# The last three modulation vectors of a DiT layer as products on ScalarE and sums on GpSimd

## The chip, the cores and the metric

The kernel runs on one core of one Trainium2 chip. The metric is the time of one execution on the device in microseconds (us). TensorE multiplies matrices, VectorE and ScalarE work on rows of up to 128 partitions, GpSimd (POOL in the profile) does element-wise work here, and SyncE (SP) issues nearly all DMAs. Each engine executes its own list of instructions in order.

## What is computed

One layer of a diffusion backbone: a feed-forward sublayer (FFN), a mixer (a gated delta rule beside windowed attention), and a second FFN, each with a norm that is shifted, scaled and gated by modulation vectors. Two groups of tokens go through it, 128 of a prompt and 512 of a sample, each with its own conditioning vector. All data is fp32. What the change touches:

```python
mod_p = (jax.nn.silu(c_ctx) @ ada_w[l] + ada_b[l])[None, None, :]
mod_s = (jax.nn.silu(c) @ ada_w[l] + ada_b[l])[:, None, :]
sh1p, sc1p, g1p, sh2p, sc2p, g2p, sh3p, sc3p, g3p = jnp.split(mod_p, N_MOD, axis=-1)
...
xp = ffn_sublayer(xp, norm_ffn1[l], sh1p, sc1p, g1p, ffn1_w13[l], ffn1_w2[l])
...
xp = xp + g2p * merge_branches(y_a, y_b, gate_raw, w_oa[l], w_ob[l], w_out[l])
xp = ffn_sublayer(xp, norm_ffn2[l], sh3p, sc3p, g3p, ffn2_w13[l], ffn2_w2[l])
```

`ada_w` has 1024 rows and 9 x 1024 columns, 4 MB for each of the nine vectors. Vectors 0 and 1 (shift and scale of the first FFN) are needed at once, 2 after the first round, 3 and 4 before the mixer, 5 at its end, and 6, 7 and 8 only in the second FFN.

## The kernel before

The FFN (`ffn`) has 22 column tiles f of 128 columns, in six rounds (0-2, 3-6, 7-10, 11-13, 14-17, 18-21). In a round each column tile makes one tile of the hidden layer, and then the second product runs over eight output tiles d and adds to the residual `X` (L455). The column tiles from f = 3 on use `product_pair` (L203): two weight blocks a and b of 512 KB are loaded (`load`, L115, three `wraw` buffers), GpSimd makes four sums and differences of their halves (`ss`, L580 to L583, four buffers), and each weight is split into a high part on ScalarE (`wh` or `sh`, L127) and a rest on VectorE (`wl` or `sl`, L128). Then seven products of twelve matmuls run over 320 columns each: 84 matmuls to a pair. In the names below, `big` and `aux` are PSUM tiles (two and four).

The modulation vectors 2 to 8 are made by a generator (`rest`, with `modulation`) that `ffn` advances through `between`: by two steps behind each of the first two column tiles, by one behind every other, and by one behind each four output tiles d in the rounds but the last. A step loads two blocks of 128 rows x 1024 columns (`araw`, L273, 512 KB each, a ring of two buffers), multiplies them with the 32 columns that repeat the two conditioning vectors (`s32`), and adds the result to `modr` (L286, L288):

```python
for g in range(4):
    nc.tensor.matmul(
        ps[32 * g : 32 * g + 32],
        lhsT=self.s32[:, k, :],
        rhs=raw[:, g * 256 : (g + 1) * 256],
```

The four matmuls of a block write four strips of 32 rows of one PSUM tile. The trace counts each of them as two instructions (two passes). After four steps a vector is complete and is transposed (L292), given its bias and kept in `mod` (L293). The 28 steps end in the fifth round. A scheduler writes the order of each engine's instructions from the order in the code, priorities and its own model of times; on the chip each engine follows that list and waits for semaphores.

Of the kernel before, what the change touches and what calls it, by code (L numbers as in the profile page):

```python
# [10 lines left out]
F32 = mybir.dt.float32  # L11
# [3 lines left out]
AF = mybir.ActivationFunctionType  # L15
ALU = mybir.AluOpType
# [3 lines left out]
P = 128  # L20
D = 1024
# [65 lines left out]
def flat(t):  # L87
    return t.rearrange("p a b -> p (a b)")
# [10 lines left out]
class Net:  # L99
# [147 lines left out]
    def vectors(self):  # L247
        nc = self.nc
        c = self.const
        ps = self.aux_tile()  # L250
        nc.tensor.transpose(ps[:, 0:16], self.crows, self.ident[0:16, 0:16])
        sT = self.tile(c, [P, 16], F32, "sT")
        nc.scalar.activation(sT, ps[:, 0:16], AF.Silu)
        self.s32 = self.tile(c, [P, KD, 32], F32, "s32")
        for v in range(2):
            nc.vector.tensor_copy(
                self.s32.rearrange("p k (r v) -> p v k r", v=2)[:, v],
                sT[:, v * 8 : v * 8 + 8].unsqueeze(2).to_broadcast([P, KD, 16]),
            )
        ps = self.aux_tile()  # L260
        nc.tensor.transpose(ps[:, 0:105], self.vrows[0:105], self.ident[0:105, 0:105])
        self.vecT = self.tile(c, [P, 105], F32, "vecT")
        nc.vector.tensor_copy(self.vecT, ps[:, 0:105])
        self.mod = self.tile(c, [P, 9, KD, 2], F32, "mod")

    def modulation(self, m):


        nc, a = self.nc, self.a
        r = self.tile(self.small, [P, 256], F32, "modr", 2)  # L270
        for k in range(KD):
            raw = self.tile(self.apool, [P, D], F32, "araw", 2)
            nc.sync.dma_start(raw, a["ada_w"][0, k * P : (k + 1) * P, m * D : (m + 1) * D])  # L273
            if k % 2 == 0:
                ps = self.aux_tile()[:, 0:256]
# [5 lines that stand above are left out]
                    start=(k % 2 == 0),  # L281
                    stop=(k % 2 == 1),
                )
            if k % 2:
                if k == 1:
                    nc.vector.tensor_copy(r, ps)  # L286
                else:
                    nc.vector.tensor_tensor(r, r, ps, op=ALU.add)  # L288
                yield
        p2 = self.aux_tile()  # L290
        for h in range(2):
            nc.tensor.transpose(p2[:, h * P : (h + 1) * P], r[:, h * P : (h + 1) * P], self.ident)  # L292
        nc.vector.tensor_tensor(  # L293
            self.mod[:, m].rearrange("p (g h) v -> p g h v", h=2),
            p2[:, 0:256].rearrange("p (h g r) -> p g h r", h=2, g=4)[:, :, :, 0:2],
            self.vecT[:, m * 8 : m * 8 + 8]
            .rearrange("p (g h) -> p g h", h=2)
            .unsqueeze(3)
            .to_broadcast([P, 4, 2, 2]),
            op=ALU.add,  # L300
        )

    def modulation_part(self, m0, d0, nd):

# [1121 lines left out]
    def build(self):  # L1426
        nc, a, tc = self.nc, self.a, self.tc
# [4 lines left out]
        def pool(name, **k):  # L1432
            return tc.tile_pool(name=name, bufs=1, reuse_waits="tile", **k)

        def dram(shape, tag):
            return self.tile(self.dram, shape, F32, tag)

        with (
# [9 lines left out]
            with (  # L1448
# [7 lines left out]
                with pool("ada0", side="right") as ada, ExitStack() as inner:  # L1456
                    with pool("in1", side="right") as self.phase:
                        self.load_input(xall, ss)
                        r = self.token_rstd(ss)
# [50 lines left out]
                with pool("g1", side="right") as self.phase:  # L1510
                    gates = {m: self.tile(self.const, [P, KD, 2], F32, f"gate{m}") for m in (2, 5, 8)}

                    def rest():
                        for m in range(2, 9):
                            yield from self.modulation(m)
                            if m in gates:
                                nc.vector.tensor_scalar(gates[m], self.mod[:, m], 0.5, None, op0=ALU.mult)
                        self.scale_columns(4, 80, A2)
                        self.scale_columns(7, 88, A3)
                        self.constants_late()  # L1520

                    A2, A3 = (self.tile(self.const, [P, KD, 2], F32, tag) for tag in ("A2", "A3"))
                    steps = rest()

                    def between(n):
                        for _ in range(n):
                            next(steps, None)

                    last = self.ffn(hs, X, gates[2], a["ffn1_w13"][0], a["ffn1_w2"][0], self.phase, between=between, first=first)
                    hs = self.next_operands(last, X, A2, 3)  # L1530
                    xd = dram([KD, P, T], "xd")
                    for d in range(KD):
                        nc.sync.dma_start(xd[d], flat(X[d]))


            with ExitStack() as right:
# [8 lines left out]
                with pool("mixt") as tmp, pool("attn") as at:  # L1545
# [29 lines left out]
                rest = [  # L1575
                    lambda off=off, chain=chain: list(chain(self.product(self.wcols(a["w_in"][0], off), hs)))
                    for off, chain in zs[2:]
                ]

                op = right.enter_context(pool("o", side="right"))  # L1580
                self.oT = self.tile(op, [P, H_A, T], F32, "oT")
                with pool("prep") as pp, pool("scan") as sp:
                    self.delta(pp, sp, rest)
                    self.nfill, self.fill = 160, 0
                    self.gates(stage, hs, range(16))
                    yB = []
                    for r in range(4):
                        t = self.tile(stage, [P, 2, HT], F32, "stage", 2)
                        nc.sync.dma_start(flat(t), ybd[r])
                        yB.append(self.operand(t, self.operand_tiles(1)[0]))  # L1590
                    tB = self.branch_b(stage, yB)
                    self.nfill = 0
# [11 lines left out]
                with pool("x2") as xpool:  # L1604
# [13 lines left out]
                    with pool("g2", side="right") as self.phase:  # L1618
                        last = self.ffn(hs, X, gates[8], a["ffn2_w13"][0], a["ffn2_w2"][0], self.phase, weight=self.vecT[:, 97:105])
                        acc = next(last)  # L1620
# [36 lines left out]
```

## Time and profile before

| | |
|---|---|
| median of 3 runs | 1578.33 us (1575.17 to 1578.99) |
| the profiled execution | 1579.08 us |
| its span in the profile | 1577.4 us |
| mean granted TensorE clock | 0.989 of full speed (2.4 GHz) |
| first FFN with its modulation steps, about | 50 to 485 us of the span |
| second FFN, about | 1150 to 1560 us of the span |

A view of the profile names an instruction by line, engine, operation and tiles (out<-in). PE is TensorE's matmul, PEld its weight load, DVE VectorE, ACT ScalarE, SPq the DMA queue of SyncE. The chain of waits is the chain of work that ended last, followed back from the end of the program.

### The profile page before, as it was taken

To read this page: it belongs to the slowest core of one execution; us is meant where nothing else is said; L and a number is where in the kernel's file an instruction comes from. 1 tells how busy PE (TensorE), PEld (TensorE's weight loads), DVE (VectorE), ACT (ScalarE), POOL (GpSimd) and SP (SyncE) were. 2 spreads that over 40 slices of the span, in tenths; PEclk is the share of its full clock that TensorE was granted. 3 is DMA by queue.
4 is the path that set the end of the run, shared out by engine and by line. 5 is a ranking of instruction groups with operands and counts; after the bars stand their busy time and mean duration, and the time that the engine had idled before them with its cause. 6 is when DMAs were issued, how large, how long until landed. Compare 5 with 4: busy or idle time off the path is not lost.

```text
span 1577.4 us, 28409 instructions
## 1 busy us (share of the span) xinstructions
PE 1537.0 (97%) x11210; PEld 1458.9 (92%) x11210; DVE 1091.9 (69%) x2309; ACT 657.7 (42%) x1214; POOL 293.6 (19%) x240
## 2 busy tenths in 40 slices
PE   6999999999999899999999999999999999999998
PEld 4889999989999798788999999999899999999997
DVE  5877575658576758976765655765698776677676
ACT  4434232324243546564455544323353333334244
POOL 1022221222220110100321122000014141241410
PEclk8999999999999999999999999999999999999999
DMA  9654354445325341214533323445022313223122
GB/s 304 206 170 160 129 173 146 134 146 170 94 80 137 93 129 44 66 41 126 177 111 98 103 80 123 152 140 164 24 75 73 116 57 109 68 68 107 55 81 67
DMA packets 219119, 181.15 MB, mean 115 GB/s; under 512 B 16032, under 2 KB 194397, under 8 KB 218987
## 3 DMA queue, kind: packets, MB, share of 16 engines
q1 hardware_dynamic: 218731, 179.29, 37.2%
q8 instruction: 88, 1.44, 0.4%
q14 instruction: 44, 0.36, 0.1%
q0 software_dynamic: 256, 0.06, 0.0%
HBM read 161.59 MB, written 16.42 MB: 113 GB/s over the span
## 4 chain that ended last, share of the span: by engine, by line
PE 84%; DVE 7%; DMA 3%; ACT 2%; issue 2%; POOL 1%; SPq 0%; DVEq 0%; POOLq 0%; ACTq 0%
PE big L173 31%; PE aux L203 21%; PE aux L173 10%; PE aux L160 9%; PE big L203 8%; DMA wraw<-ffn_w 2%; DVE wl L128 1%; PE aux L277 1%; DVE x L455 1%; PE aux L157 1%; DVE sl L128 1%; ACT wh L127 1%; DVE cacc L870 1%; PE aux L317 1%; POOL ss L580 1%
## 5 line engine op out<-in xcount | busy, mean ns | idle before, releaser
L127 ACT CAST wh<-wraw 128x1024 fp32r<-128x1024 f32 (+1 forms) x147 | 150.6, 1027 | 270.0 <-PE big L173 89.9
L128 DVE TENSOR_TENSOR wl<-wraw,wh 128x1024 fp32r<-128x1024 f32 (+1 forms) x147 | 183.0, 1247 | 84.1 <-ACT wh L127 80.9
L173 PE MATMUL big<-hh,wh 128*128 128x320 f32 x768 | 192.9, 322 | 8.7 <-ACT hh L351 3.3
L173 PE MATMUL big<-hl,wh 128*128 128x320 f32 x768 | 192.3, 321 | 0.6 <-DVE hl L420 0.5
L173 PE MATMUL big<-hh,wl 128*128 128x320 f32 x768 | 188.1, 318 | 0.5 <-DVE wl L128 0.4
L580 POOL TENSOR_TENSOR ss<-wraw 128x512 f32<-128x512 f32 x38 | 51.2, 1349 | 725.3 <-DMA wraw<-ffn_w 648.6
L127 ACT CAST sh<-ss 128x512 fp32r<-128x512 f32 x152 | 92.7, 620 | 186.1 <-POOL ss L581 89.2
L128 DVE TENSOR_TENSOR sl<-ss,sh 128x512 fp32r<-128x512 f32 x152 | 133.2, 884 | 44.6 <-ACT sh L127 43.8
L173 PEld LDWEIGHTS big<-hh,wh 128*128 128x128 f32 x768 | 131.1, 191 | 15.1 <-ACT hh L351 5.5
L203 PE MATMUL aux<-th,sh 128*128 128x320 f32 x456 | 141.7, 311 | 2.2 <-DVE x L455 2.2
L203 PE MATMUL aux<-tl,sh 128*128 128x320 f32 x456 | 141.5, 310 | 0.0
L203 PE MATMUL aux<-th,sl 128*128 128x320 f32 x456 | 141.4, 310 | 0.0
L173 PEld LDWEIGHTS big<-hl,wh 128*128 128x128 f32 x768 | 131.3, 191 | 6.6 <-DVE hl L420 3.3
L173 PEld LDWEIGHTS big<-hh,wl 128*128 128x128 f32 x768 | 131.9, 191 | 3.3 <-issue 2.2
L455 DVE SCALAR_TENSOR_TENSOR x<-big,gate,x 128x128 f32<-128x128 f32 (+2 forms) x181 | 67.5, 424 | 36.4 <-PE big L173 36.1
L203 PEld LDWEIGHTS aux<-th,sh 128*128 128x128 f32 x456 | 86.2, 189 | 2.7 <-DVE x L455 2.7
L173 PE MATMUL big<-gh,wh 128*128 128x320 f32 x352 | 88.5, 313 | 0.0
L173 PE MATMUL big<-gl,wh 128*128 128x320 f32 x352 | 87.7, 310 | 0.0
L173 PE MATMUL big<-gh,wl 128*128 128x320 f32 x352 | 87.1, 309 | 0.0
L203 PEld LDWEIGHTS aux<-tl,sh 128*128 128x128 f32 x456 | 86.2, 189 | 0.0
L203 PEld LDWEIGHTS aux<-th,sl 128*128 128x128 f32 x456 | 86.2, 189 | 0.0
L1066 DVE TENSOR_TENSOR P<-aux,lv 128x512 f16<-128x512 f32 x70 | 48.2, 689 | 46.8 <-PE aux L160 46.8
(378 smaller groups left out, 3919.4 us busy)
## 6 DMA issues: line engine op xcount, KB each, us to landing
wraw<-ffn_w SPq DMA_DIRECT2D x116, 512.0 KB, 4.0
araw<-ada_w SPq DMA_DIRECT2D x64, 512.0 KB, 5.7
wraw<-w_in SPq DMA_DIRECT2D x35, 512.0 KB, 4.0
wraw<-ffn_w SPq DMA_DIRECT2D x16, 384.0 KB, 3.3
gd<-stage SPq DMA_DIRECT2D x16, 320.0 KB, 2.7
araw<-ada_w SPq DMA_DIRECT2D x16, 256.0 KB, 6.0
wraw<-w_out SPq DMA_DIRECT2D x8, 512.0 KB, 4.2
xd<-x SPq DMA_DIRECT2D x8, 320.0 KB, 2.2
```

The costliest lines, as they stand in the source:

```text
L127: nc.scalar.copy(hi, raw)
L128: nc.vector.tensor_sub(lo, raw, hi.bitcast(F32))
L157: self.marks.append(self.nc.tensor.transpose(*args))
L160: self.marks.append(self.nc.tensor.matmul(*args, **kw))
L173: self.nc.tensor.matmul(ps[h], lhsT=wt[:, k, c0 : c0 + P], rhs=xt[:, h, :], start=(k == 0 and j == 0), stop=(k == len(xs) - 1 and j == 2),)
L203: nc.tensor.matmul(ps, lhsT=wt[:, k * P : (k + 1) * P], rhs=xt, start=(k == 0 and j == 0), stop=(k == n - 1 and j == 2),)
L277: nc.tensor.matmul(ps[32 * g : 32 * g + 32], lhsT=self.s32[:, k, :], rhs=raw[:, g * 256 : (g + 1) * 256], start=(k % 2 == 0), stop=(k % 2 ...
L317: last = nc.tensor.matmul(ps[32 * j : 32 * j + 32], lhsT=self.s32[:, 2 * q + k, :], rhs=raw[:, k, m, :], start=(q == 0), stop=(q == 3),)
L455: nc.vector.scalar_tensor_tensor(X[:, h, cols], ps[:, cols], gate[:, d, v : v + 1], X[:, h, cols], op0=ALU.mult, op1=ALU.add)
L580: nc.gpsimd.tensor_tensor(f[0], b[:, :n], b[:, n:], op=ALU.add)
L870: nc.vector.scalar_tensor_tensor(acc, buf[:, t : t + n], w, acc, op0=ALU.mult, op1=ALU.add)
L1066: mark = nc.vector.tensor_tensor(P16, p1, mask, op=ALU.mult)
```

## The change

Vectors 2 to 5 are made as before. For 6, 7 and 8 a second generator (`rest_sums`, with `modulation_sums`) runs beside the first: `between` advances it by one step whenever it is called with 1. One block g of 256 columns of a vector takes two steps; a step loads 512 rows of it as one `araw` tile (128 partitions x 4 x 256, in the same ring of two buffers). ScalarE multiplies each of the four 128 x 256 pieces by its conditioning value per partition, once for each of the two conditioning vectors, and GpSimd adds the results up in `macc`; `mprod`, which holds a product, and `macc` have one buffer each. At the end of a block TensorE sums over the 128 partitions with two matmuls (one for each conditioning vector, with a mask of zeros and ones as the stationary operand) into the strip of 32 rows of block g, VectorE copies the strip to `modr`, and the rest is as before. In the first FFN the `sh` and `sl` buffers go from six to five, as the second FFN has them already. The late constants are loaded after vector 5 instead of after vector 8.

```diff
     def modulation(self, m):
...
+        self.modulation_vector(m, r)
+
+    def modulation_vector(self, m, r):
...
+    def modulation_sums(self, m):
+        nc, a = self.nc, self.a
+        r = self.tile(self.small, [P, 256], F32, "modr", 2)
+        for g in range(4):
+            acc = self.tile(self.phase, [P, 2, 256], F32, "macc", 1)
+            for q in range(2):
+                raw = self.tile(self.apool, [P, 4, 256], F32, "araw", 2)
+                src = a["ada_w"][0, q * 512 : (q + 1) * 512, m * D + g * 256 : m * D + (g + 1) * 256]
+                nc.sync.dma_start(raw, src.rearrange("(k p) f -> p k f", p=P))
+                for k in range(4):
+                    t = acc if q == 0 and k == 0 else self.tile(self.phase, [P, 2, 256], F32, "mprod", 1)
+                    for v in range(2):
+                        nc.scalar.activation(
+                            t[:, v], raw[:, k], AF.Copy, scale=self.s32[:, 4 * q + k, v : v + 1]
+                        )
+                    if t is not acc:
+                        nc.gpsimd.tensor_tensor(acc, acc, t, op=ALU.add)
+                yield
+            ps = self.aux_tile()[:, 0:256]
+            for v in range(2):
+                nc.tensor.matmul(
+                    ps[32 * g : 32 * g + 32], lhsT=self.pick[:, v], rhs=acc[:, v], start=(v == 0), stop=(v == 1)
+                )
+            rows = slice(32 * g, 32 * g + 32)
+            nc.vector.tensor_copy(r[rows], ps[rows])
+        self.modulation_vector(m, r)
...
-                        for m in range(2, 9):
+                        for m in range(2, 6):
                             yield from self.modulation(m)
...
+                    def rest_sums():
+                        for m in range(6, 9):
+                            yield from self.modulation_sums(m)
...
                     def between(n):
                         for _ in range(n):
                             next(steps, None)
+                        if n == 1:
+                            next(sums, None)
+                    self.nsh = 5
```

Line numbers in the rows of the changed kernel are higher: L277 is the load of a modulation step, L281 its matmul, L321 the load of a sum's step, L325 a product, L329 an addition, L333 the matmul over partitions, and L617 to L620 are the four operations of a pair on GpSimd. In the waits, PE, Activation, DVE and Pool are the engines waited for; DMAHW is an earlier DMA.

SyncE in the third round (column tiles f = 8 and 9), before: two `araw` loads to a step, both waiting for TensorE.

```order
L273 DMA araw_2192<-ada_w 128x1024 [waits DMAHW4_49,DMAHW0_49,PE_49]
L273 DMA araw_2199<-ada_w 128x1024 [waits DMAHW1_49,PE_49]
L115 DMA wraw_2525<-ffn_w 128x8x128 [waits DVE_49,Pool_49]
L115 DMA wraw_2527<-ffn_w 128x8x128 [waits DMAHW2_49,DVE_49,Pool_49]
L273 DMA araw_2350<-ada_w 128x1024 [waits DMAHW4_49,PE_49]
L273 DMA araw_2357<-ada_w 128x1024 [waits DMAHW5_49,PE_49]
```

The same place now:

```order
L321 DMA araw_2373<-ada_w 128x4x256 [waits DMAHW4_49,PE_49]
L277 DMA araw_2533<-ada_w 128x1024 [waits DMAHW6_49,PE_49]
L277 DMA araw_2540<-ada_w 128x1024 [waits DMAHW2_49,DMAHW0_49,Activation_49]
L115 DMA wraw_2923<-ffn_w 128x8x128 [waits DMAHW5_49,Pool_49]
L321 DMA araw_2547<-ada_w 128x4x256 [waits DMAHW1_49,PE_49]
L277 DMA araw_2709<-ada_w 128x1024 [waits DMAHW2_49,PE_49]
```

The third load of a step (L321) has come in between, and the second load of the next modulation step waits for ScalarE, which reads the third. It is so at eleven of these loads.

TensorE at the end of a column tile of that round, before: the last matmul of a pair, the two blocks of a modulation step, the first matmul of the next pair.

```order
L203 MATMUL aux_2646<-hh_215,sh_2557 128x320
L203 MATMUL aux_2646<-hl_216,sh_2557 128x320
L203 MATMUL aux_2646<-hh_215,sl_2558 128x320
L277 MATMUL aux_2668<-araw_2666,s_32_199 32x256 x4
L277 MATMUL aux_2668<-araw_2673,s_32_199 32x256 x4
L203 MATMUL aux_2720<-hh_209,wh_2695 128x320
```

The same place now:

```order
L203 MATMUL aux_2689<-hh_219,sh_2600 128x320
L203 MATMUL aux_2689<-hl_220,sh_2600 128x320
L203 MATMUL aux_2689<-hh_219,sl_2601 128x320
L281 MATMUL aux_2711<-araw_2709,s_32_199 32x256 x4
L333 MATMUL aux_2723<-macc_2372,pick_207 32x256 x2
L281 MATMUL aux_2711<-araw_2716,s_32_199 32x256 x4
L203 MATMUL aux_2784<-hh_213,wh_2759 128x320
```

The two matmuls over partitions stand among the eight of the modulation step, ahead of the next pair.

GpSimd in that round, before: nothing but the four operations of each pair.

```order
L580 TENSOR_TENSOR ss_1770<-wraw_1768 128x512
L581 TENSOR_TENSOR ss_1771<-ss_1770,wraw_1766 128x512
L582 TENSOR_TENSOR ss_1772<-wraw_1766,wraw_1768 128x512
L583 TENSOR_TENSOR ss_1773<-wraw_1766,ss_1771 128x512
L580 TENSOR_TENSOR ss_2213<-wraw_2211 128x512
```

The same place now:

```order
L329 TENSOR_TENSOR macc_2372<-macc_2372,mprod_2549 128x512
L329 TENSOR_TENSOR macc_2372<-macc_2372,mprod_2553 128x512
L617 TENSOR_TENSOR ss_2927<-wraw_2925 128x512
L618 TENSOR_TENSOR ss_2928<-ss_2927,wraw_2923 128x512
L329 TENSOR_TENSOR macc_2372<-macc_2372,mprod_2557 128x512
L619 TENSOR_TENSOR ss_2929<-wraw_2923,wraw_2925 128x512
L329 TENSOR_TENSOR macc_2372<-macc_2372,mprod_2561 128x512
L620 TENSOR_TENSOR ss_2930<-wraw_2923,ss_2928 128x512
```

The additions of a sum's step stand between the operations of the next pairs.

## Rows read from the trace of the kernel before

**Rows 1.** The page, part 1: busy time, share of the span, instructions.

```profile
PE 1537.0 (97%) x11210; PEld 1458.9 (92%) x11210; DVE 1091.9 (69%) x2309; ACT 657.7 (42%) x1214; POOL 293.6 (19%) x240
```

**Rows 2.** The table of stretches: 50 to 485 us, busy time of each engine.

```profile
50.00:485.00 435.00, 430.11 (x3126) 407.28 (x3125) 300.58 (x560) 153.49 (x249) 102.85 (x76) 1.00 0.45 144
```

**Rows 3.** The chain of waits, third round: start us, us, engine, tile, line, matmuls.

```profile
214.95 7.23 PE aux L203 x48
222.17 3.53 PE big L203 x24
225.70 1.76 PE aux L203 x12
227.46 1.00 PE aux L277 x16
228.46 7.23 PE aux L203 x48
```

**Rows 4.** The chain of waits, second FFN: pairs without modulation steps.

```profile
1204.13 8.79 PE aux L203 x60
1212.92 3.53 PE big L203 x24
1216.45 8.79 PE aux L203 x60
```

**Rows 5.** The tile `araw`: durations ns min/median/max, idle before it, landing of its loads.

```profile
L277 PE MATMUL aux<-araw,s x448: 376/379/404, 48.5 to 406.1; 128*32 128x256 f32 x150
...
  DMA araw<-ada_w: 0.5, 2
...
DMA to landing us min/median/max: 2.8/5.8/11.0
```

**Rows 6.** Groups by form, ScalarE, whole run: busy us, mean ns of one, idle before.

```profile
L469 ACT ACTIVATE x<-x,vecT 128x320 f32<-128x320 f32 x16 | 9.0, 562 | 0.5
L418 ACT ACTIVATE hh<-ht,mod 128x192 fp32r<-128x192 f32 x16 | 7.3, 456 | 0.9
```

**Rows 7.** Groups by form, GpSimd, 50 to 485 us.

```profile
L583 POOL TENSOR_TENSOR ss<-wraw,ss 128x512 f32<-128x512 f32 x19 | 27.7, 1459 | 5.5 <-DVE sl L128 5.5
...
L581 POOL TENSOR_TENSOR ss<-ss,wraw 128x512 f32<-128x512 f32 x19 | 25.0, 1314 | 6.9 <-POOL ss L580 3.7 <-issue 2.2
```

**Rows 8.** The page, part 6: DMA issues, KB each, median us to landing.

```profile
wraw<-ffn_w SPq DMA_DIRECT2D x116, 512.0 KB, 4.0
araw<-ada_w SPq DMA_DIRECT2D x64, 512.0 KB, 5.7
```

**Rows 9.** The waits of the DMA queue, 0 to 480 us: total us, times, longest.

```profile
SPq L273 <- PE aux L277: 36.2, 25, 5.8
```

**Rows 10.** The chain of waits, first round: one load by itself.

```profile
69.91 3.65 DMA araw<-ada_w
```

**Rows 11.** The timeline of GpSimd, third round: start us, us, instruction.

```profile
218.74 1.29 POOL L580 TENSOR_TENSOR ss<-wraw 128x512 f32<-128x512 f32 x1 [7.02 <-DMA wraw<-ffn_w]
```

**Rows 12.** The timeline of VectorE, the same stretch.

```profile
219.20 1.39 DVE L128 TENSOR_TENSOR sl<-ss,sh 128x512 fp32r<-128x512 f32 x1
...
227.43 0.49 DVE L611 TENSOR_TENSOR s<-s,u 128x320 f32<-128x320 f32 x1 [0.26 <-ACT s L608]
...
229.24 0.49 DVE L505 TENSOR_TENSOR gl<-s,gh 128x320 fp32r<-128x320 f32 x1
...
231.25 1.22 DVE L128 TENSOR_TENSOR wl<-wraw,wh 128x1024 fp32r<-128x1024 f32 x1
...
232.78 0.69 DVE L128 TENSOR_TENSOR sl<-ss,sh 128x512 fp32r<-128x512 f32 x1
```

More of the change, by code (lines that the diff above doesn't have):

```diff
@@ L264, in vectors @@
         self.mod = self.tile(c, [P, 9, KD, 2], F32, "mod")
+        self.pick = self.tile(c, [P, 2, 32], F32, "pick")
+        nc.gpsimd.memset(self.pick, 0.0)
+        for v in range(2):
+            nc.gpsimd.memset(self.pick[:, v].rearrange("p (r v) -> p v r", v=2)[:, v], 1.0)
     def modulation(self, m):
@@ L289, in modulation @@
                 yield
+        self.modulation_vector(m, r)
+    def modulation_vector(self, m, r):
+        nc = self.nc
         p2 = self.aux_tile()
@@ L301, in modulation @@
         )
+    def modulation_sums(self, m):
[17 more added lines that the diff above has]
+            ps = self.aux_tile()[:, 0:256]
+            for v in range(2):
+                nc.tensor.matmul(
[4 more added lines that the diff above has]
+        self.modulation_vector(m, r)
     def modulation_part(self, m0, d0, nd):
@@ L1518, in rest @@
                         self.scale_columns(4, 80, A2)
+                        self.constants_late()
+                    def rest_sums():
+                        for m in range(6, 9):
+                            yield from self.modulation_sums(m)
+                            if m in gates:
+                                nc.vector.tensor_scalar(gates[m], self.mod[:, m], 0.5, None, op0=ALU.mult)
                         self.scale_columns(7, 88, A3)
-                        self.constants_late()
                     A2, A3 = (self.tile(self.const, [P, KD, 2], F32, tag) for tag in ("A2", "A3"))
-                    steps = rest()
+                    steps, sums = rest(), rest_sums()
                     def between(n):
```

## The prediction

> **What bounds the kernel now.** I read the page first, then TensorE through the stretch the change touches. TensorE is busy 97% of the span, ScalarE 42%, GpSimd 19% [rows 1]. That looks like the case for the edit: take work from the full engine, give it to two with room. The stretch table narrows it: from 50 to 485 us, nearly all of the first feed-forward layer, TensorE is idle for 435.0 - 430.1 = 4.9 us [rows 2]. So no wait worth more than 5 us can be won there; a gain has to come from TensorE doing less.
>
> The chain of waits shows what TensorE does between two column tiles: one product pair takes 7.23 + 3.53 + 1.76 = 12.52 us, then one modulation step of 16 instructions (eight matmuls in two passes each) takes 1.00 us, then the next pair starts without a gap [rows 3]. In the second feed-forward layer, which has no modulation step, a pair takes 8.79 + 3.53 = 12.32 us, gapless too [rows 4]. Modulation therefore costs 1.0 us of TensorE time per step, although each instruction is listed at 379 ns [rows 5]: 16 x 379 ns would be 6.1 us, so they run side by side.
>
> **The change, part by part.**
>
> *TensorE, removed.* Vectors 6, 7, 8 had four steps each: 12 x 1.00 us = 12.0 us.
>
> *TensorE, added.* 12 blocks of two matmuls (four passes) into one 32-row strip. No row shows a lone strip. Lower bound: if passes go out as they do now, 1.00/16 = 0.063 us each, a block costs 0.25 us. Upper bound: four passes one after another at their listed 379 ns, 1.5 us. The rows decide between them: a 320-column matmul takes 7.23/48 = 0.151 us [rows 3], 2.1 columns per ns, while a pass of 256 columns in 0.063 us would be 4.1. So one strip cannot do that; the 1.00 us is four strips at once, each doing its four passes at 0.25 us. A lone strip with four passes takes 4 x 0.25 = 1.0 us, and 12 blocks cost 12.0 us. **The TensorE term is -12.0 + 12.0 = 0** (ends: -9.0 and +6.2). Four times fewer matmuls, same time. The Trainium skill, TensorEngine Tiling (Array Packing), When to Use Tiling, says the same against this change: 32 stationary columns allow four matmuls side by side, so 96 old ones weigh as 24, and the sum by that rule is 0 too.
>
> *ScalarE, added.* 192 products of 128x256. A Copy with a column scale takes 562 ns at 320 columns, one of Identity 456 ns at 192 [rows 6]; between them, 0.51 us. 192 x 0.51 = 98 us more on an engine busy 153 of the 435 us [rows 2]: room as a total, so no term of its own.
>
> *GpSimd, added.* 84 additions of 128x512. The same shape takes 1.31 to 1.46 us there [rows 7], say 1.35: 113 us beside 103 us [rows 2]. Room as a total, too.
>
> *VectorE.* 12 copies of 32 rows for 12 adds of 128: nothing either way.
>
> *Loads.* Still eight of 512 KB per vector, in pieces of 1 KB instead of 4 KB. The weight loads, in 512-byte pieces, land in 4.0 us, the modulation loads in 5.7 [rows 8]: small pieces are not slower. No term for volume.
>
> *Five sh/sl buffers instead of six, the earlier constants, the pick masks.* The second layer runs with five and its pairs have no gap [rows 4]; the masks are three GpSimd memsets ahead of the loop. Nothing, unless POOL or VectorE falls behind, which is a rival below.
>
> *The ring of two load buffers: the term that counts.* Before, each step takes two loads, x and y, freed by TensorE right after use; SyncE waited for that 36.2 us in 25 times [rows 9] and nobody waited for SyncE: TensorE stood 0.5 us for these loads [rows 5]. Now, while both generators run, a step takes three: x and y for TensorE, z for the products. The ring has two places, so z takes the place of x, and the next y waits for **z's products on ScalarE**. Eleven y loads do (the SP order shows them with a wait on Activation). Between one step's x and the next step's y now lies a chain: load z, four pairs of products, load y.
> - Load: 5.8 us, the median [rows 5]. It may be less: one alone took 3.65 us [rows 10], the least is 2.8 [rows 5]. I take the median, since weight loads are in flight beside it.
> - Products: the product buffer is single, so ScalarE (2 x 0.51 = 1.02 us) and GpSimd (1.35 us) alternate. First half of a block: 4 x 1.02 + 2 x 1.35 = 6.8 us to the last product; second half: 4 x 1.02 + 3 x 1.35 = 8.1. Mean 7.45.
> - Sum: 5.8 + 7.45 + 5.8 = 19.05 us.
>
> TensorE's own work from one step's y to the next step's x is a pair, half a step and on average half a block: 12.3 + 0.5 + 0.5 = 13.3 us. Let d be the time from x's start to y's start within a step. The y starts at 0.5 + 19.05 after the last x, the next x at d + 13.3 after it; so two successive d add up to 0.5 + 19.05 - 13.3 = 6.25, on average 3.1 us. Half a microsecond is x's own work; **2.6 us is a stand**. Eleven times: **+29 us**. Everything else on TensorE is queued behind the waiting matmul (it executes in order), and after the wait the pair is simply later: no other engine sets the rate, so nothing wins it back.
> - Lower end: both loads at 2.8 and a first half, 12.4 us: no stand, 0.
> - Upper end: second half, with the four GpSimd subtractions of the next pair (4 x 1.35 = 5.4) all ahead of its additions: 25.1 us, stand 5.7 us, 11 x 5.7 = +62 us.
>
> I stay in the middle: the GpSimd order does put such operations inside the chain, but in some steps a block's matmuls or a part of a pair stand between x and y in TensorE's order and fill the time.
>
> *After vectors 2 to 5 are done* (from the third round's last pair on) the ring serves z alone, two buffers for a period of 12.3 + 0.5 us: no wait. A block must finish in two periods, 25.6 us: seven additions and eight subtractions, 15 x 1.35 = 20 us on GpSimd. It fits; 0 taken.
>
> **Sum.** 0 + 29 + 0 = +29 us on the profiled execution's 1579.08 us, which lies 0.75 us over the median of the runs, 1578.33: **1608 us**.
>
> **The rivals.**
>
> *A: GpSimd and VectorE get in each other's way, and the pairs stretch.* A split of 128x512 on VectorE takes 0.69 us alone and 1.39 us when it begins inside a GpSimd operation, ending 0.56 us after that one's end [rows 11, 12]. If they exclude each other wholly, a pair needs GpSimd's four subtractions and 3.5 additions (7.5 x 1.29 = 9.7 us [rows 11]) plus VectorE's operations on two SBUF inputs: five splits at 0.69, one at 1.22, two of 0.49 for the result and two more for the products [rows 12], 6.6 us. Together 16.3 us against 13.3: 3.0 us for each of 15 pairs, +45 us, 1624 us. For: the split that took twice its time [rows 12]. Against: the second layer's pairs already hold 5.2 + 6.6 = 11.8 us of the 12.3 and have no gap [rows 4], so a part of each operation may overlap. The Trainium skill, SBUF — State Buffer, Who interferes with whom, states that the two exclude each other for the whole instruction; by that rule the sum is these 1624 us.
>
> *B: faster.* One mechanism: the strip's four passes follow each other as closely as four strips' do now, 0.25 us a block, -9.0 us, and the ring chain stays at or below 13.8 us (there d is 0.5 us and nothing is waited for), as it would with loads near 3 us; 1579 - 9 = 1570 us, a little less if some of today's idling goes too. Decides: the duration of a block and the landing time of z. Against: 4.1 columns per ns, which no row shows.
>
> *C: no change.* The strip costs 1.0 us and the chain is hidden, because z is loaded and multiplied early: 1579 us, within 4.7 us. For: TensorE stood 0.5 us for such loads so far [rows 5]. Against: y's place in the order.
>
> **How the numbers follow.** My forecast of 1608 us (1590 to 1630) gets 0.55, A (1624, up to 1645) 0.22, B 0.12, C 0.11. The first two are slower: 0.77. About 0.3%, 4.7 us, is what a measurement of this kernel tells from no change. The range has to reach C and the edge of B, and most of A: 1575 to 1640 us; outside it lie some 0.10 of B and 0.07 of A.
>
> **What would show it.** Right: 24 new matmuls in 12 groups of about 1.0 us; idle time of TensorE before the old modulation matmuls of some 2 to 3 us each, released by the load, whose issue on SP waited for ScalarE; all of it between about 85 and 300 us; pairs after that near 12.8 us a period without gaps. If GpSimd's contention were the cause, the idle time would stand before the pair's own matmuls, released by VectorE's sl, up to 420 us. Wrong: a new group of 0.25 us, or no idle time before the modulation matmuls; then the price of the strip or the length of the chain was mistaken.

## The result, and the profile after

| | before | after |
|---|---|---|
| median (4 runs each, same chip) | 1577.70 us | 1657.10 us (1654.22 to 1659.90) |
| span of the profiled execution | 1577.4 us | 1657.0 us |
| TensorE busy over the span | 1537.0 us | 1560.3 us |
| TensorE idle (span less busy) | 40.4 us | 96.7 us |
| mean granted TensorE clock | 0.989 | 0.971 |

The ratio is 1.0501, 95% interval 1.0483 to 1.0519: 79 us slower, where 29 were forecast, and outside the range. Of the 79.6 us between the two spans, 56.3 are new idle time of TensorE and 23.3 are a longer busy time for work that by the forecast costs the same.

The page of the changed kernel: busy times (against [rows 1]), and the chain's shares by engine and line.

```profile
PE 1560.3 (94%) x11066; PEld 1470.1 (89%) x11066; DVE 1122.3 (68%) x2309; ACT 736.2 (44%) x1406; POOL 413.1 (25%) x327
...
PE 70%; DVE 8%; POOL 7%; ACT 6%; DMA 5%; issue 4%; SPq 0%; POOLq 0%; DVEq 0%; ACTq 0%
```

The loss is over before the part of the mixer in which GpSimd runs one operation ten times (tile `E`; behind the durations stand the first and the last start), before and then after:

```profile
L1091 POOL TENSOR_TENSOR E<-ident,U x10: 1273/1289/2043, 796.2 to 970.2; 128x512 f32<-128x512 f32 x10
```

```profile
L1128 POOL TENSOR_TENSOR E<-ident,U x10: 1277/1293/2042, 873.1 to 1046.9; 128x512 f32<-128x512 f32 x10
```

First and last start both shift by 77 us. So the stretch to look at is 50 to 570 us, the first FFN with what follows it; its row in the table of stretches (length, then PE, PEld, DVE, ACT, POOL, granted clock, DMA share, GB/s), before and after:

```profile
50.00:570.00 520.00, 509.95 (x3635) 483.49 (x3634) 356.01 (x696) 191.10 (x322) 113.16 (x90) 0.99 0.45 140
```

```profile
50.00:570.00 520.00, 459.79 (x3026) 425.31 (x3015) 334.67 (x564) 234.20 (x446) 222.85 (x160) 0.94 0.40 121
```

TensorE's idle time goes from 10.1 to 60.2 us and its clock from 0.99 to 0.94. What ended that idle time, after (TensorE's waits in the stretch: total us, times, longest):

```profile
PE aux L333 <- POOL macc L329: 16.0, 3, 7.5
PE big L173 <- ACT gh L541: 15.3, 4, 7.0
PE aux L281 <- DMA araw<-ada_w: 14.2, 7, 5.4
PE aux L203 <- DVE u L649: 4.7, 3, 2.0
```

Only the third line is the wait that the forecast was made of. The first is TensorE reaching a block's two matmuls before GpSimd has finished the block's sum. The second is TensorE waiting for a pair's own result, and two of its stands, 7.0 and 6.7 us, lie behind 380 us, where the two generators no longer share the ring (the last L281 starts at 285.9 us).

**One stand read through the engines' lists.** TensorE, timeline (start us, us, instruction, idle before and releaser):

```profile
390.28 0.63 PE L173 MATMUL big<-gh,wh 128*128 128x320 f32 x1 [7.00 <-ACT gh L541]
```

GpSimd up to there:

```profile
376.16 1.30 POOL L329 TENSOR_TENSOR macc<-macc,mprod 128x512 f32<-128x512 f32 x1 [1.09 <-ACT mprod L325]
378.55 1.30 POOL L329 TENSOR_TENSOR macc<-macc,mprod 128x512 f32<-128x512 f32 x1 [1.09 <-ACT mprod L325]
380.94 1.29 POOL L329 TENSOR_TENSOR macc<-macc,mprod 128x512 f32<-128x512 f32 x1 [1.08 <-ACT mprod L325]
382.19 1.29 POOL L617 TENSOR_TENSOR ss<-wraw 128x512 f32<-128x512 f32 x1
383.56 1.26 POOL L618 TENSOR_TENSOR ss<-ss,wraw 128x512 f32<-128x512 f32 x1
384.77 1.27 POOL L619 TENSOR_TENSOR ss<-wraw,wraw 128x512 f32<-128x512 f32 x1
386.00 1.71 POOL L329 TENSOR_TENSOR macc<-macc,mprod 128x512 f32<-128x512 f32 x1
387.67 1.71 POOL L620 TENSOR_TENSOR ss<-wraw,ss 128x512 f32<-128x512 f32 x1
```

ScalarE and VectorE:

```profile
382.26 0.91 ACT L325 ACTIVATE mprod<-araw,s 128x256 f32<-128x256 f32 x2 [1.47 <-POOL macc L329]
384.85 1.14 ACT L127 CAST sh<-ss 128x512 fp32r<-128x512 f32 x2 [1.67 <-POOL ss L618]
...
387.75 0.91 ACT L325 ACTIVATE mprod<-araw,s 128x256 f32<-128x256 f32 x2 [1.12 <-POOL macc L329]
388.56 0.60 ACT L127 CAST sh<-ss 128x512 fp32r<-128x512 f32 x1
389.77 0.46 ACT L541 CAST gh<-s 128x320 fp32r<-128x320 f32 x1 [0.60 <-DVE s L648]
```

```profile
385.50 2.76 DVE L128 TENSOR_TENSOR sl<-ss,sh 128x512 fp32r<-128x512 f32 x2 [4.92 <-ACT sh L127]
388.18 1.55 DVE L648 TENSOR_TENSOR s<-s,u 128x320 f32<-128x320 f32 x1
```

Read them from the bottom. TensorE needs `gh` of the pair's result; ScalarE makes it as soon as VectorE's product L648 ends. L648 stands in VectorE's list behind two splits `sl`; these wait 4.92 us for `sh`, `sh` waits for the *next* pair's subtraction L618, and the subtractions stand in GpSimd's list behind the additions. Those come at 2.4 us each, because GpSimd waits 1.1 us for every product and ScalarE 1.47 us for every addition (there is one product buffer). GpSimd's gap is too short for a subtraction of 1.3 us, and in its fixed order the subtraction does not come until the addition ahead of it has run. ScalarE's list does the same to the pair: the cast at 388.56 us, of a subtraction that had ended at 386.04, stands behind a product that waits 1.12 us for GpSimd. Then the two-input operations of VectorE run long beside GpSimd: the two splits take 2.76 us for 2 x 0.69, L648 takes 1.55 for 0.49 [rows 12]. The splits run beside an addition and a subtraction, L648 beside L620 alone, a subtraction that has come late. So one stand shows two causes, **turns** and **contention**, and neither is on TensorE.

How far GpSimd has fallen behind is seen in the idle time ahead of a pair's first subtraction, 85 to 530 us, before and after (groups: busy, mean ns, idle before and what ended it):

```profile
L580 POOL TENSOR_TENSOR ss<-wraw 128x512 f32<-128x512 f32 x19 | 26.0, 1367 | 332.6 <-DMA wraw<-ffn_w 300.9 <-DVE modr L288 31.7
```

```profile
L617 POOL TENSOR_TENSOR ss<-wraw 128x512 f32<-128x512 f32 x18 | 26.9, 1494 | 57.9 <-DVE sl L128 18.1 <-DMA wraw<-ffn_w 14.8 <-DVE modr L337 13.0
```

Before, GpSimd stood 301 us there waiting for weights; after, 15. It went from an engine that waits for its data to one for which the data wait, though it is busy only 223 of 520 us.

**The clock.** TensorE's timeline after a stand of 3.4 us, and at a block without one:

```profile
121.82 1.91 PE L333 MATMUL aux<-macc,pick 128*32 128x256 f32 x4 [3.44 <-POOL macc L329]
123.66 0.64 PE L203 MATMUL aux<-hh,wh 128*128 128x320 f32 x1
124.10 0.47 PE L203 MATMUL aux<-hl,wh 128*128 128x320 f32 x1
124.36 0.47 PE L203 MATMUL aux<-hh,wl 128*128 128x320 f32 x1
...
334.92 1.05 PE L333 MATMUL aux<-macc,pick 128*32 128x256 f32 x4
335.90 0.41 PE L203 MATMUL aux<-hh,wh 128*128 128x320 f32 x1
336.15 0.31 PE L203 MATMUL aux<-hl,wh 128*128 128x320 f32 x1
336.30 0.31 PE L203 MATMUL aux<-hh,wl 128*128 128x320 f32 x1
```

The same two stretches in the table of stretches:

```profile
118.00:126.00 8.00, 4.56 (x21) 2.87 (x14) 2.90 (x5) 0.97 (x2) 3.77 (x3) 0.71 0.59 199
330.00:338.00 8.00, 8.00 (x53) 7.18 (x52) 6.55 (x13) 1.99 (x4) 2.64 (x3) 1.00 0.45 131
```

Behind the stand the pair's matmuls start 0.26 us apart, without one 0.15 us; the granted clock is 0.71 in the first stretch, part of which ran at the lower of the two levels (1.2 GHz), and 1.00 in the second. The lower level follows the stand, and the same block takes 1.91 us instead of 1.0. So a long stand is paid a second time in slow matmuls. An estimate from the two rows of 50 to 570 us: a clock lower by 0.05 for 520 us is 26 us of full-speed time, a part of it idle; the 23 us of longer busy time are of that size.

### The profile page after: what moved, and what is told of

Same layout as the page of the kernel before. It is cut to its first block, busy times and chain, and to the rows that moved or that the text cites. A ratio compares the mean times of both kernels' runs of the same rounds, so it can differ in the third digit from the quotient of the medians.

```text
span 1657.0 us, 28500 instructions
## 1 busy us (share of the span) xinstructions
PE 1560.3 (94%) x11066; PEld 1470.1 (89%) x11066; DVE 1122.3 (68%) x2309; ACT 736.2 (44%) x1406; POOL 413.1 (25%) x327
## 4 chain that ended last, share of the span: by engine, by line
PE 70%; DVE 8%; POOL 7%; ACT 6%; DMA 5%; issue 4%; SPq 0%; POOLq 0%; DVEq 0%; ACTq 0%
PE big L173 31%; PE aux L203 11%; PE aux L173 10%; PE aux L160 9%; POOL macc L329 4%; PE big L203 4%; DMA wraw<-ffn_w 3%; ACT mprod L325 2%; DMA araw<-ada_w 1%; DVE wl L128 1%; DVE sl L128 1%; ACT wh L127 1%; POOL ss L620 1%; POOL ss L618 1%; PE aux L157 1%
## 5 line engine op out<-in xcount | busy, mean ns | idle before, releaser
L128 DVE TENSOR_TENSOR sl<-ss,sh 128x512 fp32r<-128x512 f32 x152 | 143.6, 951 | 54.8 <-ACT sh L127 54.0
L329 POOL TENSOR_TENSOR macc<-macc,mprod 128x512 f32<-128x512 f32 x84 | 114.4, 1362 | 237.8 <-ACT mprod L325 201.3
L617 POOL TENSOR_TENSOR ss<-wraw 128x512 f32<-128x512 f32 x38 | 54.9, 1444 | 458.5 <-DMA wraw<-ffn_w 337.0
L325 ACT ACTIVATE mprod<-araw,s 128x256 f32<-128x256 f32 x168 | 76.6, 502 | 99.7 <-POOL macc L329 90.6
L173 PE MATMUL big<-gh,wh 128*128 128x320 f32 x352 | 91.7, 322 | 15.3 <-ACT gh L541 15.3
L173 PE MATMUL big<-gl,wh 128*128 128x320 f32 x352 | 91.2, 319 | 0.8 <-DVE gl L542 0.8
```

What stands on the lines that cost most here:

```text
L128: nc.vector.tensor_sub(lo, raw, hi.bitcast(F32))
L173: self.nc.tensor.matmul(ps[h], lhsT=wt[:, k, c0 : c0 + P], rhs=xt[:, h, :], start=(k == 0 and j == 0), stop=(k == len(xs) - 1 and j == 2),)
L325: nc.scalar.activation(t[:, v], raw[:, k], AF.Copy, scale=self.s32[:, 4 * q + k, v : v + 1])
L329: nc.gpsimd.tensor_tensor(acc, acc, t, op=ALU.add)
L617: nc.gpsimd.tensor_tensor(f[0], b[:, :n], b[:, n:], op=ALU.add)
```

## The experiments

Times are medians; each is compared with the kernel before on the same chip. "Idle" and "busy" are TensorE's over the span of the profile.

| run | what it is | difference, us | ratio, 95% interval | idle, busy us |
|---|---|---|---|---|
| before | | 0 | | 40.4, 1537.0 |
| after | the change | +79.4 | 1.0483 to 1.0519 | 96.7, 1560.3 |
| e1_no_adds | change, products only | +20.0 | 1.0091 to 1.0169 | 52.7, 1539.9 |
| e2_adds_only | change, additions only | +55.1 | 1.0323 to 1.0383 | 83.2, 1547.9 |
| e4_halves | change, two half product buffers | +52.7 | 1.0307 to 1.0367 | 79.4, 1549.2 |
| e11_change_memset | change, fills for additions | +47.9 | 1.0276 to 1.0336 | 70.4, 1553.5 |
| e3_sums_after | later placement, two vectors | +51.1 | 1.0297 to 1.0357 | 81.0, 1545.8 |
| e7_after_no_adds | e3, products only | +3.5 | 1.0004 to 1.0027 | 47.9, 1534.1 |
| e8_after_adds_only | e3, additions only | +20.2 | 1.0082 to 1.0165 | 54.9, 1539.7 |
| e9_after_halves | e3, two half product buffers | +28.6 | 1.0143 to 1.0221 | 65.1, 1537.6 |
| e10_turns_memset | e3, fills for additions | +21.3 | 1.0106 to 1.0165 | 56.0, 1541.8 |
| e12_halves_memset | e9, fills for additions | +12.8 | 1.0054 to 1.0112 | 51.9, 1537.4 |
| e5_pool_only | before, with extra additions | +84.0 | 1.0488 to 1.0567 | 107.7, 1554.9 |
| e6_act_only | before, with extra products | +6.0 | 1.0028 to 1.0060 | 42.6, 1537.3 |

### Taking the additions or the products away

e1_no_adds keeps loads, ring, products and strip, and drops the additions:

```diff
-                    if t is not acc:
-                        nc.gpsimd.tensor_tensor(acc, acc, t, op=ALU.add)
```

> Products on ScalarE as in the change, but the 84 GpSimd additions are left out (a block's sum is its first product alone, so vectors 6 to 8 come out wrong). Handshake theory (products and additions take turns at 2.4 us a pair, ScalarE's list stands behind GpSimd, and TensorE behind both): ScalarE never waits for GpSimd, so nearly all of the +79 us goes: 1580 to 1595 us, TensorE idle from 50 us to the end of the first FFN below 20 us. Ring theory (the two load buffers alone): products of 4 us and two loads still lie between, half of the waits on the modulation loads stay and with them some 1610 us or more. Contention theory (GpSimd's additions slow VectorE): also near 1580 to 1595, so this run alone does not part it from the handshake.

e2_adds_only keeps the first product of a block, and adds the loaded rows themselves for the rest:

```diff
-                    t = acc if q == 0 and k == 0 else self.tile(self.phase, [P, 2, 256], F32, "mprod", 1)
...
+                    else:
+                        nc.gpsimd.tensor_tensor(
+                            acc, acc, raw[:, k].unsqueeze(1).to_broadcast([P, 2, 256]), op=ALU.add
+                        )
```

> The other half: the 84 additions stay on GpSimd, of the same shape, but they add the loaded weights themselves; ScalarE makes only the first product of each block (vectors 6 to 8 come out wrong). Handshake theory: ScalarE stands behind GpSimd no more, 1585 to 1610 us. Contention theory: GpSimd's load is that of the change, so the time stays at 1640 to 1660 us. Ring theory: additions of 4 x 1.3 us still hold the load buffer, 1610 us or more.

Measured: +20.0 us (1596.77) and +55.1 us (1631.86). e1 lies 2 us above the range of the handshake theory. e2 misses that range and the one of contention; of the three, only the ring's "1610 us or more" holds it. Without additions 59 of the 79 us are gone, and so is most of the clock's loss (busy 1539.9 us for the same instructions on TensorE). Without most of the products the time falls by 24 us only. TensorE's waits for the ring, e1 and then e2:

```profile
PE aux L281 <- DMA araw<-ada_w: 9.6, 7, 3.8
```

```profile
PE aux L281 <- DMA araw<-ada_w: 27.1, 10, 5.1
```

The ring's wait is real in all of these, and it follows the engine that frees the buffers: short when the products free them, long when GpSimd's additions do. In the change it is 14.2 of 56.3 us of new idle time, but in e1 it is 9.6 of 12.3 and in e2 27.1 of 42.8, the larger part in both.

### Taking the ring away

e3_sums_after starts the sums when the older generator has ended, so that the ring serves one of them at a time; there is room for vectors 6 and 7 only.

```diff
-                        for m in range(6, 9):
+                        for m in range(6, 8):
...
-                            next(steps, None)
-                        if n == 1:
-                            next(sums, None)
+                            if next(steps, self) is self:
+                                next(sums, None)
```

> The sums start only when the old generator has finished (vector 5 done), so that the ring of two buffers never serves both; since fewer calls are left, only vectors 6 and 7 are made (16 of the 24 steps), vector 8 is set to one. Ring theory: no modulation load waits for ScalarE any more, 1575 to 1590 us. Handshake theory: the stretch from 300 to 500 us of the changed kernel, where the ring serves the sums alone, holds about 10 steps and cost some 40 us, 4 us a step; 16 steps cost about 65 us: 1625 to 1650 us.

```profile
PE big L173 <- ACT gh L541: 23.4, 3, 8.8
PE aux L203 <- DVE u L649: 6.1, 3, 3.1
```

Measured: +51.1 us for 16 of the 24 steps, inside the handshake's range and far from the ring's, while TensorE waits no more than 0.4 us for the ring's loads. This is the run that fells a term of the forecast: in the phase where I had taken 0, the change costs two thirds of its price. The wait is the one traced above, for the pair's own result.

e7_after_no_adds and e8_after_adds_only make the cuts of e1 and e2 in this placement.

> Sums started after the old generator (vectors 6 and 7 alone, vector 8 set to one), products on ScalarE, no additions: neither the shared ring nor GpSimd. Ring theory and handshake theory: 1572 to 1585 us; if it stays above 1595, the products in ScalarE's list cost by themselves.

> Sums started after the old generator (vectors 6 and 7 alone, vector 8 set to one), additions on GpSimd that read the loaded weights, ScalarE only for the first product of a block: GpSimd's additions without the shared ring and nearly without the turns. Contention theory: 1600 to 1625 us, close to the 1628 us of the same with products. Handshake theory: 1575 to 1590 us.

Measured: products alone +3.5 us, additions alone +20.2, both +51.1. e8, at 1598.51 us, lies between the ranges of the two theories. The parts do not add up, 24 against 51; what only the two together have is the hand-over between ScalarE and GpSimd. One reservation holds for all these runs: each edit is scheduled anew, so GpSimd's order is not held. Of the 19 pairs in 50 to 570 us, additions stand inside the four subtractions of 11 in the change, 10 in e11, 9 in e4 and 3 in e2; in the later placement of 5 in e3, e9 and e10, 6 in e12 and 2 in e8. So additions alone also stood less in the way of the pairs.

### Loading one engine of the kernel before

e6_act_only adds eight products of 128x256 to each of 24 steps of the kernel before (five sh/sl buffers as in the change), nobody reads them; e5_pool_only adds four additions of 128x512 in the same places.

```diff
+                        if n == 1 and next(extra, None) is not None:
+                            for _ in range(4):
+                                for v in range(2):
+                                    nc.scalar.activation(acc[:, v], other[:, v], AF.Copy, scale=self.s32[:, 0, v : v + 1])
```

> The kernel before, with five sh/sl buffers and 192 products of 128x256 on ScalarE (eight behind each of the 24) that nobody reads: ScalarE's load of the change by itself. All theories: 1577 to 1585 us; above 1590 the products' mere place in ScalarE's list, ahead of the pair's copies and casts, would be a cost of its own.

> The kernel before, with five sh/sl buffers and 96 additions of 128x512 on GpSimd (four behind each of 24 column tiles or groups of output tiles) whose result nobody reads: GpSimd's load of the change by itself, with no load buffer, no product and no waiting matmul. Contention theory (GpSimd takes SBUF time from VectorE and delays the pairs): 1600 to 1625 us. Ring and handshake theory: 1577 to 1585 us, since nobody waits for these additions.

e6: +6.0 us. ScalarE does have the room, as long as its products wait for nobody; all of them lie between 56 and 187 us, closer together than in the change. e5: +84.0, outside both ranges, and it does not test what it was made for. With nothing to wait for, the additions were put early into GpSimd's order in bursts, one of 18 between the last operation of a pair and the first of the next (timeline of GpSimd):

```profile
144.34 1.74 POOL L583 TENSOR_TENSOR ss<-wraw,ss 128x512 f32<-128x512 f32 x1
146.05 28.51 POOL L1537 TENSOR_TENSOR macc<-macc,mprod 128x512 f32<-128x512 f32 x18
174.51 1.26 POOL L580 TENSOR_TENSOR ss<-wraw 128x512 f32<-128x512 f32 x1
```

The next pair's subtraction starts the moment the burst of 28.5 us ends. It shows what work ahead of a pair costs in GpSimd's list, and leaves contention open.

### Two half buffers: the turns loosened

e4_halves (in the change) and e9_after_halves (in the later placement) cut the product buffer into two of 1 KB, so that ScalarE fills one while GpSimd adds the other:

```diff
-                    t = acc if q == 0 and k == 0 else self.tile(self.phase, [P, 2, 256], F32, "mprod", 1)
...
+                        t = acc[:, v] if new else self.tile(self.phase, [P, 256], F32, "mprod", 2)
...
+                            nc.gpsimd.tensor_tensor(acc[:, v], acc[:, v], t, op=ALU.add)
```

> The same arithmetic, with the product tile of 2 KB cut into two buffers of 1 KB, one for each conditioning vector, and 168 additions of 128x256 instead of 84 of 128x512: ScalarE can make the next half while GpSimd adds the last. Handshake theory: a pair of products with its additions takes about 1.4 us instead of 2.4, so the waits shrink: 1610 to 1640 us. Contention theory: GpSimd is busy as long or longer, 1655 to 1670 us.

> The kernel with the two sums placed after the older generator (vectors 6 and 7 by the new way, vector 8 set to one and not computed), and its one product buffer of 2 KB cut into two of 1 KB, so that ScalarE can write one half-product while GpSimd adds the other; 112 additions of 128x256 in the place of 56 of 128x512. With whole products this placement took about 51 us over the kernel before; additions without products took about 20, products without additions about 3. Theory (ScalarE and GpSimd take turns through one buffer, and the pair's copy, silu and GpSimd work queue behind the turns): the overlap takes most of the difference away, about 1600 us (1592 to 1610). Rival (it is the time that GpSimd holds the memory beside VectorE): GpSimd's time grows from 75 to 97 us by these additions, so no gain, 1628 us or more.

Measured: +52.7 for +79.4, and +28.6 for +51.1; e9 lies in the theory's bounds. GpSimd is busier by it, 247 us against 223 in the stretch 50 to 570 us of e4, and the kernel faster by 27 us: it is not GpSimd's work but its waiting in turns that costs these. In e4 the wait of L333 for the sum is gone too. What is left in e4 is for the most part the ring: TensorE's wait for its loads has grown from 14.2 to 23.5 us, of 39.0 us of new idle time.

```profile
PE aux L281 <- DMA araw<-ada_w: 23.5, 9, 8.1
```

e4 is the fastest form found that computes everything; none came near the kernel before.

### Fills: the reads taken away

e10_turns_memset, e11_change_memset and e12_halves_memset replace each addition by fills of the product buffer, which take about as long on GpSimd (0.52 + 0.52 + 0.31 us for an addition of 1.34; in e12 0.31 + 0.31 + 0.15 for a half addition of 0.83) and keep the turns, but read nothing. They also leave the sum `macc` alone, so L333 no longer waits for GpSimd. The edit of e10 and e11; e12 fills `t`, `t` and `t[:, 0:64]`:

```diff
-                        nc.gpsimd.tensor_tensor(acc, acc, t, op=ALU.add)
+                        [nc.gpsimd.memset(z, 0.0) for z in (t, t, t[:, 0])]
```

> The same placement (vectors 6 and 7 by the new way, vector 8 not computed), whole products in one buffer, but each addition is replaced by three fills of the product buffer on GpSimd (two of 128x512, one of 128x256, about 1.3 us together by the time of the fill of 128x648), so the turns between ScalarE and GpSimd stay and the additions' two reads go; the sums are wrong by it. Theory (the turns make the time): 1610 us or more, as long as the fills take about the addition's time. Rival (the additions slow VectorE by reading memory beside it): VectorE's weight subtraction falls back to its time in the kernel before, and the time to about 1582 to 1590 us.

> The fourth corner: sums after the older generator (vectors 6 and 7, vector 8 not computed), two product buffers of 1 KB and fills in the place of the 112 half additions (two of 128x256 and one of 128x64 each, about 0.7 us), so neither the strict turns nor the additions' reads; the sums are wrong by it. If turns and reads are the two causes, little is left: 1580 to 1590 us. If GpSimd's time in its in-order list alone costs something (the pair's subtractions queue behind the sums), 1595 us or more.

> The change itself, all three vectors by the new way and between the older steps, with each addition replaced by three fills of the product buffer on GpSimd (1.36 us together in the run before, an addition 1.34), so the ring of two load buffers, the strip and the turns stay and the additions' reads go; vectors 6 to 8 are wrong by it. Reading so far: in the later placement turns alone cost about 21 us, reads alone about 20, both about 51, so the reads cost about 30 for 56 additions beside the turns. If that holds here for 84, some 45 us of the change's 79 go: about 1612 us (1600 to 1625). Rival (here the turns and the load ring hold the time, and the reads only lengthen what is hidden): 1635 us or more.

e10 came between the two bounds, at 1599.62 us: each theory held a part. VectorE's `gl`, two inputs of 128x320 (min/median/max ns), in 85 to 530 us of the kernel before, the change and e11:

```profile
L505 DVE TENSOR_TENSOR gl<-s,gh x40: 483/487/495, 87.4 to 486.6; 128x320 fp32r<-128x320 f32 x40
```

```profile
L542 DVE TENSOR_TENSOR gl<-s,gh x33: 475/479/1565, 88.8 to 529.9; 128x320 fp32r<-128x320 f32 x33
```

```profile
L542 DVE TENSOR_TENSOR gl<-s,gh x38: 469/485/494, 89.6 to 520.9; 128x320 fp32r<-128x320 f32 x38
```

In the change some take up to 1.57 us, in e11 none more than 0.49. But two long ones of the change, merged in one row of VectorE's timeline, and GpSimd's timeline beside them show that the addition need not be the partner:

```profile
483.11 2.85 DVE L542 TENSOR_TENSOR gl<-s,gh 128x320 fp32r<-128x320 f32 x2
482.53 1.59 POOL L617 TENSOR_TENSOR ss<-wraw 128x512 f32<-128x512 f32 x1 [0.30 <-DMA wraw<-ffn_w]
484.20 1.41 POOL L618 TENSOR_TENSOR ss<-ss,wraw 128x512 f32<-128x512 f32 x1
```

They run beside the pair's own subtractions. Take all of VectorE's operations in that stretch that make `gl` from `s` and `gh` or `s` from `s` and `u` (two inputs of 128x320). Before, 1 of 78 overlaps with an operation of GpSimd; in the change 23 of 65 do: 5 with additions alone (up to 1.58 us), 15 with the pair's subtractions alone (up to 1.58), 3 with both. In e11, 26 overlap with fills alone and none of them takes more than 0.49 us, while 13 overlap with subtractions and take up to 1.59. So fills do leave VectorE alone, and a good part of the change's contention is with subtractions that come late. VectorE's busy time over the whole span says the same: 1091.9 us before, 1122.3 in the change, 1093.1 in e11.

The four corners of the later placement:

| | fills | additions |
|---|---|---|
| two half buffers | +12.8 | +28.6 |
| one buffer, strict turns | +21.3 | +51.1 |

The reads cost 16 us with loose turns and 30 with strict ones; the turns cost 9 with fills and 23 with additions. Each corner is known to some 5 us. They make each other worse, as in the stand above, where a late split then also ran long. e12 (1590.55 us, just over the bound of the theory) leaves 9 us over e7 for GpSimd's time in its list and what turns are left. In the change itself e11 gives +47.9 us, just over the range of the theory: 31 of the 79 us go, not 45. Not all of the 31 are shown to be the reads: L333's wait for the sum, 16.0 us in the change, went with them, since the fills do not write `macc`. In the later placement neither e3 nor e10 has that wait, so the 30 us there are free of it.

That divides the change, one step upon the other: products, loads, ring and strip +20 (e1); GpSimd's time in its list and the turns +28 (e11 less e1); the additions' reads, with the wait for the sum, +31 (the change less e11). Each step holds its share of the slower clock.

## Why the prediction was wrong

- **TensorE's term, 0: right.** The 48 listed passes come in 12 groups of four, and a group takes 0.98 us at the full clock (334.92 to 335.90 us). The Trainium skill, TensorEngine Tiling (Array Packing), When to Use Tiling, was cited for this, and the trace agrees. Rival B, a strip of 0.25 us, is out. In e7 the new way costs 3.5 us more than the old one even with no additions at all and one vector fewer, so nothing was to be won.
- **The ring, +29: right in kind, half in size.** The waits are where the forecast put them, and SyncE waits for ScalarE's products (77.1 us in 10 times before L277). TensorE stands 14.2 us for these loads in 7 stands, mean 2.0 us, where eleven of 2.6 were forecast. The mis-sized term is in part the load: `araw` loads land in 4.6 us (median, 50 to 300 us), where 5.8 was taken twice; by the forecast's own sum that makes 1.4 us a stand, 16 us for eleven, an estimate. The term moves with what stands beside it: 9.6 us in e1, 23.5 in e4, 27.1 in e2.
- **"A block must finish in two periods, 25.6 us: ... 20 us on GpSimd. It fits; 0 taken": the step that failed.** It adds up GpSimd's busy time. The section on the ring had the price of a turn, 1.02 + 1.35 = 2.37 us, and the trace shows just that: additions at 376.16, 378.55 and 380.94 us, 2.4 apart. But it was used for the ring alone. Seven turns are 16.6 us, and GpSimd's 1.1 us between two additions holds no subtraction of 1.3; with eight subtractions at 1.35 a block asks up to 27.4 us of GpSimd's list, an estimate, where 25.6 were allowed. Measured, the matmuls of successive blocks stand 31.9 us apart in e3 and 27.5 in e7, which has no additions. e3 measures this phase by itself: +51 us, where 0 was taken, and 30 of them go when the additions are replaced by fills (e10). The forecast's sign, pairs without gaps after 300 us, is missed: stands of 7.0 and 6.7 us end at 390 and 483 us.
- **"Room as a total, so no term of its own": the same fault on ScalarE.** e6 shows that the room exists (+6.0 us). What ScalarE lost is its order: casts and copies of the pair stand behind a product that waits for GpSimd.
- **"No other engine sets the rate, so nothing wins it back":** half true. Nothing won it back, but GpSimd's list came to hold TensorE up, for the block's sum (L333, 16.0 us) and by way of VectorE and ScalarE for `gh` (15.3 us).
- **Rival A, +45: a real cause, a part of the time.** The reads cost 30 us in the later placement (e3 less e10) and at most 31 in the change (e11), and VectorE's products take up to three times as long; its splits take 1.03 us in the mean for 0.90 before (85 to 530 us). Its sign in the trace is there in part: idle time stands before the pair's own matmuls, but up to 483 us, not 420, and released by ScalarE's `gh` (15.3 us), by `sl` only 1.2 us. That fills leave VectorE alone agrees with the Trainium skill, SBUF — State Buffer, Who interferes with whom: an operation of VectorE with two inputs collides with GpSimd instructions that read, not with those that only write; e11's 26 overlaps with fills, none above 0.49 us, bear it out. The 1624 us worked out from whole exclusion are not the time, since the turns were missing in it.
- **The clock was in no term.** Stands were priced once. TensorE's busy time rose by 23.3 us, of the 79.6; with e1's products alone it rose by 2.9.

What stays open: how e1's 20 us divide. e7 has the five sh/sl buffers, the earlier constants, products and strips too, for two vectors, and costs 3.5 us, so most of the 20 comes with sharing the ring and the place between the older steps; TensorE's stands for the loads are 9.6 us of it. Open too: how much of the change's 31 us is the reads and how much the wait for the sum; how much the order, made anew for each run, adds to each difference; and what two whole product buffers would give.

## What to carry to other kernels

When work is moved to two engines that hand it to each other through one buffer, price the turn (both durations together) and lay the turns into each engine's order beside what is already there; the sum of busy times says nothing about whether it fits. An engine that is 19% busy may have no slack at all where its results are due, so look at what ends the idle time before its operations: GpSimd's 301 us of waiting for weights were this kernel's head start, and the change spent them. And before moving work off TensorE, count what is left there: a narrow strip took as long as the four it replaced. And when one wait is loosened, look for the one behind it: with two half buffers the wait for the ring grew from 14 to 24 us.

## What the runs showed of the hardware

- A stand of TensorE is paid twice. After idle times of 3.4 to 7 us its matmuls run at half the clock for a while: 56 us of new idle time came with 23 us of longer busy time.
- GpSimd's additions and subtractions of 128x512 and VectorE's operations on two SBUF inputs lengthen each other, both ways: L650 (`s`, at 433 us) from 0.49 to 1.58 us beside an addition, `gl` to 1.57 beside subtractions, an addition from 1.26 to as much as 2.24 (at 120 us, beside a split `wl`). Fills on GpSimd leave VectorE at 0.49 (26 overlaps in e11).
- Splitting an addition of 128x512 (mean 1.36 us) into two of 128x256 (0.86 us each in e4) makes GpSimd busier and this kernel faster, since the other engine can work meanwhile.
